# Layer 1's V stage with the expert weights as the moving operand: 128 tokens wide, 32 tokens in four column groups, every second tile as three fp32r products

## The chip, the cores and the metric

The kernel runs on one core of a Trainium2 chip. The core has five engines with queues of their own: TensorE (matmuls into PSUM, called PE in the profile, its weight loads PEld), VectorE (DVE), ScalarE (ACT), GpSimd (POOL) and SyncE (SP), and 16 DMA engines that move data between the chip's memory and SBUF. The metric is the time of one execution in microseconds, as the median of several runs. Everything is f32 unless said otherwise; a matmul on f32 operands leaves two records of TensorE in the trace, one on fp32r operands (f32 rounded so that one pass does it) leaves one.

## The reference, cut to what matters

Two layers; each is a mixer (convolution and attention, not touched here) and then a layer of experts. For each of 272 tokens a router picks 8 x 16 = 128 of 16384 experts. An expert is a row of `u` and a row of `v`, of 1024 numbers each:

```python
def block(args):
    xb, ib, wb = args
    a = jnp.einsum('ted,td->te', u_table[ib], xb)
    act = jax.nn.gelu(a) * wb
    return jnp.einsum('te,ted->td', act, v_table[ib])
...
h = h + _peer(_rmsnorm(h, ffn_norm_g[l]), peer_wq[l], peer_keys[l], peer_u[l], peer_v[l])
...
return h[:, N_META:]
```

The output is the last layer's `h` without the 16 meta tokens: 256 tokens of 1024 numbers.

## The kernel before

**Two ways for the experts.** In each layer a part of the tokens takes the sparse way: for each of them (a job) POOL gathers its 128 rows of `u` and `v` (1 MB) into a buffer `gb`, one of four; VectorE multiplies by the token and sums (L1385), ACT applies gelu and the weight (L1395, L1396), and VectorE adds the weighted `v` rows to `va` (L1371), one job later. Layer 1 has 96 such jobs, in groups of 64 and 32 tokens (`toks`). The other N = 160 tokens (d0 = 112 to 271) take the dense way: all 16384 experts are computed. The U stage multiplies 128 tiles of `u` by the tokens and applies gelu and the routing weights; its result is X and Xh, for each tile j of 128 experts a block `xj(j)` of 128 experts x 160 tokens. The V stage multiplies X by `v`: 128 tiles j of 128 experts x 1024 outputs.

**The V stage.** For each tile j it runs eight matmuls, one for each block c of 128 output columns: the stationary operand is `w_[:, c*128:(c+1)*128]`, a piece of `v`, the moving operand is `xj(j)`, 160 tokens, and the result is added up in PSUM with outputs on partitions and tokens along the row (`pov`, in four tiles `po`). 124 tiles run in a loop; the last four (LJ = 124 to 127) are kept for the end, where they run block by block, so that each block of outputs can be finished while the next is multiplied. In layer 1 a finished block is added to the residual `hT` on VectorE (L1501), turned by two TensorE transposes (L1482), copied out of PSUM (L1487, L1489) and written to `out` in pieces of 128 KB.

**Weights.** All weight tiles come in one order, two tiles j in each transfer of 1 MB, through a ring of four buffers `wraw` (RAW = 4). SP issues a transfer when TensorE is done with the buffer that it overwrites (`dma_to`, L87). `next_w` hands out the next tile, `peek_w(n)` looks n tiles ahead.

**Order.** The order on every engine is that in which the code is written. Between the matmuls of two tiles, `some_gathers(rv)` advances the sparse jobs by a fixed number of steps, three steps to a job; rv is chosen so that the jobs of the layer run out three tiles before the loop's end. In the V stage a gather is issued behind a tiny POOL copy (`warm`, L1359) that waits for the weights of the current tile to land. When a group of sparse tokens is done, `sum_heads` adds up its partial sums by eight matmuls with `zs_` (a matrix that sums partitions) into PSUM `xp`, and `put_back` adds these to `hT`.

**Three products.** Earlier stages already use this: `high` copies a weight tile to fp32r on ACT (L674), `low` subtracts that from the tile on VectorE (L684), and `three` multiplies high by high, low by high and high by low.

Of the kernel before, what the change touches and what calls it, by code (L numbers as in the profile page):

```python
# [7 lines left out]
F32 = mybir.dt.float32  # L8
F32R = mybir.dt.float32r
# [28 lines left out]
GB = 4  # L38
LASTP = 2
# [11 lines left out]
def trunk_kernel(ctx: ExitStack, tc: tile.TileContext, a: dict, out: bass.AP, dbg=None, stop=None):  # L51
    nc = tc.nc
    V, S, G, PE = nc.vector, nc.scalar, nc.gpsimd, nc.tensor

    ctx.enter_context(tc.manual_schedule())
    pp = ctx.enter_context(tc.tile_pool(name="persist", bufs=1))

    def mm(o, l, r, start, stop):
        PE.matmul(o, l, r, start=start, stop=stop, skip_group_check=True)  # L59
# [12 lines left out]
    RAW = 4  # L72
    raws = {}
    first = []
    state = {"dma": 0, "use": 0}
    n_l = len(srcs) // NL
    early_ = [[l * n_l + 30 + p for p in EARLY] for l in range(NL)]
    ring = [k for k in range(len(srcs)) if k not in early_[0] + early_[1]]

    def dma_to(n):  # L80
        while state["dma"] < min(n, len(ring)):
            k = ring[state["dma"]]
            r = pp.tile([128, 2, 1024], F32, name="wraw", bufs=RAW)
            if k == 0:
                first.append(r)
            else:
                nc.sync.dma_start(r, srcs[k])  # L87
# [34 lines left out]
    ident = pp.tile([128, 128], F32, name="ident")  # L122
# [29 lines left out]
    zs_ = {}  # L152
# [10 lines left out]
    def run_all(g):  # L163
        for _ in g:
            pass
# [32 lines left out]
    for l in range(NL):  # L198
        last = l == NL - 1
# [59 lines left out]
        else:  # L259

            p = zp.tile([128, 512], F32, name="z", bufs=3)
# [499 lines left out]
        w_, z = next_w(), zp.tile([128, 512], F32, name="z", bufs=3)[:, :T]  # L761
# [118 lines left out]
        xh = pp.tile([128, 8, T], F32, name="xh").bitcast(F32R)  # L880
# [22 lines left out]
        xp = (xh, xl)  # L903
# [196 lines left out]
        toks = [(META + sum(GROUPS[l][:g]), n) for g, n in enumerate(GROUPS[l])] + ([] if last else [(0, 16)])  # L1100
# [16 lines left out]
        xh = pp.tile([128, 8, T], F32, name="xh")  # L1117
        for i in range(16):
# [9 lines left out]
            if i % 3 == 1:  # L1128
                k = next(ahead, None)
# [33 lines left out]
            if 4 <= i < 12:  # L1163
                c = i - 4
# [184 lines left out]
        def gathers():  # L1349

            bufs = {}

            def gather(k):
                if k < len(jobs):
                    i, m = jobs[k]
                    g_ = bufs[k] = gp.tile([128, 2048], F32, name="gb", bufs=GB)
                    if done["v"]:

                        G.tensor_copy(warm[0:1], state["w"][0:1, 0:1])  # L1359
                    G.indirect_dma_start(out=g_, out_offset=None, in_=a[f"uv{l}"],  # L1360
                                         in_offset=bass.IndirectOffsetOnAxis(
                                             ap=iww[i].bitcast(I32)[:, m // 16, 0, m % 16:m % 16 + 1], axis=0))

            def add(i, m, r):
                s_ = m % 16
                m_ = am[i][:, m // 16, s_:s_ + 1]
                if m == 0:
                    vac[i] = gp.tile([128, 1024], F32, name="va", bufs=2)
                    V.tensor_scalar(vac[i], r, m_, None, op0=OP.mult)
                else:  # L1370
                    V.scalar_tensor_tensor(vac[i], r, m_, vac[i], op0=OP.mult, op1=OP.add)  # L1371

            for k in range(GB):
                gather(k)
            yield from x_steps(0)
            nx = iter(())
            for k, (i, m) in enumerate(jobs):
                if m == 4 and i + 1 < len(toks):
                    nx = x_steps(i + 1)
                if m in (4, 10):  # L1380
                    next(nx, None)
                g_ = bufs.pop(k)
                u_, r = g_[:, 0:1024], g_[:, 1024:]
                m_ = am[i][:, m // 16, m % 16:m % 16 + 1]
                V.scalar_tensor_tensor(u_, u_, 1.0, xrs[i], op0=OP.mult, op1=OP.mult, accum_out=m_)  # L1385
                yield
                if k:
                    add(*prev)
                    gather(k - 1 + GB)
                    if m == 3 and i:  # L1390
                        sum_heads(i - 1)
                    if m == 5 and i:
                        put_back(i - 1)
                yield
                S.activation(m_, m_, AF.Gelu_apprx_tanh)  # L1395
                S.activation(m_, m_, AF.Copy, scale=iww[i][:, m // 16, 1, m % 16:m % 16 + 1])  # L1396
                prev = (i, m, r)
                yield
            add(*prev)
# [57 lines left out]
        LJ = 128 - 2 * LASTP  # L1457
        tail = 3
        rv = (3 * nj + 3 - done["n"] - 3 * tail) / (LJ - tail)
        pos = [pV.tile([128, 512], F32, name=f"po{i}") for i in range(4)]  # L1460
        pov = [pos[3 - c // 2][:, c % 2 * 256:c % 2 * 256 + N] for c in range(8)]
        for j in range(LJ):
            w_ = next_w()
            for c in range(8):
                mm(pov[c], w_[:, c * 128:(c + 1) * 128], xj(j), j == 0 and c % 2 == 0, False)
            some_gathers(rv if j < LJ - tail else 3)
        run_all(gs_)
        vs2.close()

        ws_ = [next_w() for _ in range(2 * LASTP)]  # L1470
        if last:
            ov = out.rearrange("o (t p) d -> p (o t) d", p=128)
            ms = ExitStack()
            pm = ms.enter_context(tc.tile_pool(name=f"pm{l}", bufs=1, space=PSUM))
            turned = []

            def turn_out(c):

                if c % 2 == 0:
                    turned[:] = [pm.tile([128, 512], F32, name="pt", bufs=2)[:, 0:256] for _ in range(2)]  # L1480
                for t in range(2):
                    PE.transpose(turned[t][:, c % 2 * 128:c % 2 * 128 + 128], hT[:, c, 16 + t * 128:144 + t * 128], ident)  # L1482
                if c % 2:
                    for t in range(2):
                        ob = gp.tile([128, 2048], F32, name="gb", bufs=GB)[:, 0:256]
                        if t:
                            S.activation(ob, turned[t], AF.Copy)  # L1487
                        else:
                            V.tensor_copy(ob, turned[t])  # L1489
                        (S if t else nc.sync).dma_start(ov[:, t, c // 2 * 256:c // 2 * 256 + 256], ob)  # L1490

        for c in range(8):
            if c == (1 if last else 5):
                sum_heads(len(toks) - 1)
                put_back(len(toks) - 1)
            for j in range(LJ, 128):
                mm(pov[c], ws_[j - LJ][:, c * 128:(c + 1) * 128], xj(j), False, j == 127)
            if last:
                if c > 1:
                    turn_out(c - 2)  # L1500
                V.tensor_add(hT[:, c, d0:], hT[:, c, d0:], pov[c])  # L1501
        if last:
            turn_out(6)
            turn_out(7)
            ms.close()
        else:
            carry = (pov, vs, d0)
        mts.close()
        xhs.close()
        if last:  # L1510
            vs.close()
# [82 lines left out]
```

## Time and profile before

| | us |
|---|---|
| median of three runs (1714.29 to 1715.16) | 1714.66 |
| the profiled execution | 1712.8 |
| its span, first to last instruction | 1711.0 |
| TensorE busy | 1676.9 (98%) |
| VectorE busy | 1163.2 (68%) |
| ScalarE busy | 575.9 (34%) |
| layer 1's V stage, from the first `po` matmul | 1421.57 |
| last copy out of PSUM ends | 1707.85 |

How to read the rows further down: a row of a window gives the stretch, its length, each engine's busy time with its number of records, the clock that TensorE was granted (1.00 is full), the share of time in which the 16 DMA engines were busy, and GB/s. A row of a timeline gives start, duration, engine, line, operation, output<-inputs, shapes and count; neighbours of one kind are merged. In rows on waits stand who waited for whom, the sum in us, how often, and the longest. In groups stand `busy us, mean ns` behind the bar. L59 is the line of the helper through which all matmuls go, so matmuls are told apart by the names of their tiles. The ends of matmuls are modelled, so their pace is read from starts.

### The profile page before, as it was taken

The page shows a single profiled execution, that of the slowest core. Times are in us where ns is not written, and L with a number is a line of the kernel's source. Part 1 is how long each engine was busy: PE and PEld are TensorE (multiplying, and loading weights), DVE is VectorE, ACT ScalarE, POOL GpSimd, SP SyncE. Part 2 cuts the span into 40 slices and gives each one's busy share as a digit, 9 for nine tenths or more (in the row PEclk, how much of TensorE's full clock was granted, in tenths as well). Part 3 has the DMA queues.
Part 4 walks back from the last instruction along what each step waited for, and adds up shares of the span by engine and source line. Part 5 has one row for each costly group of instructions (what it writes and reads, how often), then busy time and mean ns, then how long its engine had stood idle before and what let it go on. Part 6 is the DMA issues. An engine that isn't in the chain of part 4 may idle for free.

```text
span 1711.0 us, 30698 instructions
## 1 busy us (share of the span) xinstructions
PE 1676.9 (98%) x12067; PEld 1593.6 (93%) x12067; DVE 1163.2 (68%) x3005; ACT 575.9 (34%) x1632; POOL 300.4 (18%) x352
## 2 busy tenths in 40 slices
PE   9999999989999999999999989999999999999998
PEld 7688989989999999998986889999999999999998
DVE  6789888888888544444447898888788885333333
ACT  3475623335544111000024666333355441000000
POOL 0000013222112213222300100122221112222120
PEclk9999999999999999999999999999999999999999
DMA  6344777999999999999962556889999999999995
GB/s 241 109 138 160 249 230 304 363 382 420 421 420 420 420 420 415 421 420 412 416 250 98 137 165 246 256 330 360 411 421 423 423 416 419 385 382 391 400 392 203
DMA packets 85520, 568.51 MB, mean 332 GB/s; under 512 B 9592, under 2 KB 14904, under 8 KB 18168
## 3 DMA queue, kind: packets, MB, share of 16 engines
q1 hardware_dynamic: 49776, 338.54, 50.1%
q0 software_dynamic: 34880, 227.41, 34.5%
q8 instruction: 95, 1.56, 0.4%
q10 hardware_dynamic: 720, 0.60, 0.1%
q14 instruction: 49, 0.40, 0.1%
HBM read 556.18 MB, written 1.05 MB: 326 GB/s over the span
## 4 chain that ended last, share of the span: by engine, by line
PE 66%; DMA 10%; DVE 9%; issue 9%; ACT 2%; POOL 2%; POOLq 0%; SPq 0%; DVEq 0%; ACTq 0%
PE po L59 27%; PE A L59 16%; PE z L59 16%; DMA wraw<-vn 6%; DMA gb<-uv,iww 4%; PE aps L59 3%; POOL gb L1360 2%; PE wp L59 1%; DVE va L1371 1%; DVE gb L1385 1%; PE sc L59 1%; PE xp L59 1%; DVE acc L626 0%; DVE xh L684 0%; DVE kh L684 0%
## 5 line engine op out<-in xcount | busy, mean ns | idle before, releaser
L59 PE MATMUL A<-xh,wraw 128*128 128x160 f32 x3776 | 534.8, 301 | 1.2 <-ACT idxT L990 1.2
L1385 DVE SCALAR_TENSOR_TENSOR gb<-gb,xr 128x1024 f32<-128x1024 f32 x208 | 254.6, 1224 | 396.5 <-DMA gb<-uv,iww 396.2
L59 PEld LDWEIGHTS A<-xh,wraw 128*128 128x128 f32 x3776 | 517.7, 191 | 1.6 <-issue 1.6
L1360 POOL DMA_INDIRECT gb<-uv,iww x208 | 225.1, 1082 | 528.5 <-DVE va L1371 381.5
L59 PE MATMUL po<-Xh,wraw 128*128 128x160 f32 x2080 | 286.9, 300 | 3.9 <-DMA wraw<-vn 3.3
L59 PEld LDWEIGHTS po<-Xh,wraw 128*128 128x128 f32 x2080 | 283.1, 190 | 6.6 <-DMA wraw<-vn 5.3
L59 PE MATMUL po<-X,wraw 128*128 128x160 f32 x2016 | 277.1, 300 | 6.5 <-DMA wraw<-vn 3.6
L59 PEld LDWEIGHTS po<-X,wraw 128*128 128x128 f32 x2016 | 274.2, 190 | 8.9 <-DMA wraw<-vn 5.8
L1371 DVE SCALAR_TENSOR_TENSOR va<-gb,am,va 128x1024 f32<-128x1024 f32 x203 | 260.0, 1281 | 1.7 <-ACT am L1396 1.5
L1395 ACT ACTIVATE am<-am 128x1 f32<-128x1 f32 x208 | 41.3, 198 | 591.0 <-DVE gb L1385 590.9
L59 PE MATMUL z<-xg,wraw 128*128 128x272 f32 (+2 forms) x960 | 223.5, 391 | 0.1
L59 PEld LDWEIGHTS z<-xg,wraw 128*128 128x128 f32 (+1 forms) x960 | 175.0, 188 | 38.8 <-issue 5.8
L1299 ACT ACTIVATE ohA<-ohE,wlo 128x128 f16<-128x128 f16 x320 | 105.2, 429 | 6.7 <-DVE ohE L1296 5.9
L1359 POOL COPY warm<-wraw 1x1 f32<-1x1 f32 x86 | 33.2, 386 | 323.7 <-DMA wraw<-vn 323.7
L626 DVE SCALAR_TENSOR_TENSOR acc<-upad,cols,acc 128x272 f32<-128x272 f32 (+1 forms) x198 | 82.8, 487 | 0.2
L1310 ACT ACTIVATE Xh<-wp 128x260 f32<-128x260 f32 (+18 forms) x80 | 25.0, 312 | 125.5 <-DVE Xh L1307 111.1
L1396 ACT ACTIVATE am<-am,iww 128x1 f32<-128x1 f32 x208 | 61.3, 295 | 6.8
L1296 DVE TENSOR_TENSOR ohE<-ioh,idxT 128x512 f16<-128x512 f16 x160 | 60.4, 420 | 0.0
L638 POOL DMA_DIRECT2D part<-cp x12 | 13.2, 1102 | 254.5 <-ACT cp L635 106.6
L59 PE MATMUL wp<-ohE,ohA 128*128 128x128 f16 x640 | 51.1, 219 | 1.8 <-DVE ohA L1297 1.8
L59 PEld LDWEIGHTS <-ohA 128*128 128x128 f16 x640 | 43.2, 97 | 7.0 <-DVE ohA L1297 2.8
L59 PE MATMUL A<-xh,we 128*128 128x160 f32 x320 | 45.3, 299 | 0.0
(423 smaller groups left out, 1912.0 us busy)
## 6 DMA issues: line engine op xcount, KB each, us to landing
wraw<-vn SPq DMA_DIRECT2D x128, 1024.0 KB
wraw<-u SPq DMA_DIRECT2D x118, 1024.0 KB
wraw<-w_in SPq DMA_DIRECT2D x27, 1024.0 KB
wraw<-wq SPq DMA_DIRECT2D x16, 1024.0 KB
we<-u SPq DMA_DIRECT2D x10, 1024.0 KB
wraw<-w_out SPq DMA_DIRECT2D x8, 1024.0 KB
wraw<-w_mla SPq DMA_DIRECT2D x4, 1024.0 KB
wraw<-w_conv SPq DMA_DIRECT2D x4, 1024.0 KB
```

Source lines behind the costliest of these rows:

```text
L59: PE.matmul(o, l, r, start=start, stop=stop, skip_group_check=True)
L626: V.scalar_tensor_tensor(acc[:, c, t0:], u_, weight(c, k), acc[:, c, t0:], op0=OP.mult, op1=OP.add)
L638: G.dma_start(part[:, :, t0:], u_[:, :, t0:], accum_op=OP.add)
L1296: V.tensor_tensor(E[q], ioh[:, None].to_broadcast(full), pairs(q, b), op=OP.is_equal)
L1299: S.activation(A_[1][:, t // 2, :, t % 2], E[0][:, t // 2, :, t % 2], AF.Copy, scale=wlo[:, 4 * b + t:4 * b + t + 1])
L1310: S.activation(x_, p[:, :, a:b].rearrange("p t j -> p j t"), AF.Copy, scale=1.0 / WS)
L1359: G.tensor_copy(warm[0:1], state["w"][0:1, 0:1])
L1360: G.indirect_dma_start(out=g_, out_offset=None, in_=a[f"uv{l}"], in_offset=bass.IndirectOffsetOnAxis(ap=iww[i].bitcast(I32)[:, m // 16, 0, ...
L1371: V.scalar_tensor_tensor(vac[i], r, m_, vac[i], op0=OP.mult, op1=OP.add)
L1385: V.scalar_tensor_tensor(u_, u_, 1.0, xrs[i], op0=OP.mult, op1=OP.mult, accum_out=m_)
L1395: S.activation(m_, m_, AF.Gelu_apprx_tanh)
L1396: S.activation(m_, m_, AF.Copy, scale=iww[i][:, m // 16, 1, m % 16:m % 16 + 1])
```

## The change

Layer 0 stays as it is. In layer 1's V stage the operands change places: X becomes the stationary operand and `v` the moving one, so that the result stands with tokens on partitions and outputs along the row.

- *wide*: 128 of the 160 tokens (columns 32 to 159 of `xj(j)`) are stationary, and two matmuls of 512 columns each give all 1024 outputs, into `po[0]` and `po[1]`.
- *narrow*: the other 32 tokens are stationary in four column groups, each with 256 of the 1024 outputs, into four strips of 32 partitions of `po[2]`. This is done for four tiles at a time, behind every fourth tile.
- *three parts*: every odd tile from 3 to 123 has its wide part as three fp32r products. `split`, written three tiles ahead, makes `ah` and `hi` on ACT and `al` and `lo` on VectorE; `hi` and `lo` have two sets of buffers, the storage `xh` and the new tiles `vh`, `vl`.
- *a fifth weight buffer*: every fifth `v` tile pair of layer 1 goes to `wr5` in a new pool; transfers are issued at every fourth tile.
- *the residual* is added by matmuls of `hT` with the identity, for the dense tokens in mid-loop and for the sparse ones in `give`, which takes the place of `sum_heads`; `give_out` takes that of `put_back` and writes the finished tokens to `out`.
- *the end*: the last four tiles' narrow parts, the last `give`, then the wide parts of the first and the second 512 outputs, with copies and writes behind each. There are no transposes and no additions into `hT` any more.

```diff
+            v = k - n_l * NL + 64
+            if v >= 0 and v % 5 == 4:
+                r = state["pool"].tile([128, 2, 1024], F32, name="wr5")
+            else:
+                r = pp.tile([128, 2, 1024], F32, name="wraw", bufs=RAW)
...
+            def three_parts(j):
+
+                return 3 <= j < LJ and j % 2 == 1
...
+                w_ = peek_w(2)
+                if j // 2 % 2:
+                    hi, lo = [tpp.tile([128, 1024], F32, name=x).bitcast(F32R) for x in ("vh", "vl")]
+                else:
+                    hi, lo = [axy[:, 1024 * x:1024 * x + 1024].bitcast(F32R) for x in range(2)]
+                ah, al = [tpp.tile([128, 128], F32, name=x, bufs=2).bitcast(F32R) for x in ("ah", "al")]
+                S.activation(ah, xj(j)[:, 32:160], AF.Copy)
+                S.activation(hi, w_, AF.Copy)
+                V.tensor_tensor(al, xj(j)[:, 32:160], ah.bitcast(F32), op=OP.subtract)
+                V.tensor_tensor(lo, w_, hi.bitcast(F32), op=OP.subtract)
...
+                for h in hs:
+                    mm(po[h], a_, w_[:, 512 * h:512 * h + 512], s0, end)
...
+                for g in range(4):
+                    mm(po[2][32 * g:32 * g + 32, 0:256], a_[:, 0:32], w_[:, 256 * g:256 * g + 256], s0, end)
...
+                for g in range(k):
+                    mm(p[n * g:n * g + n], zs_[n], vac[i][:, w * g:w * g + w], True, False)
+                for x in range(w // 128):
+                    for g in range(k):
+                        mm(p[n * g:n * g + n, 128 * x:128 * x + 128], hT[:, g * w // 128 + x, q0:q0 + n], ident,
+                           False, x == w // 128 - 1)
...
-            for c in range(8):
-                mm(pov[c], w_[:, c * 128:(c + 1) * 128], xj(j), j == 0 and c % 2 == 0, False)
-            some_gathers(rv if j < LJ - tail else 3)
...
+                if j % 4 == 0:
+                    dma_to(ring.index(state["use"] // 2) + RAW + 1)
+                w_ = next_w()
+                four.append((j, w_))
+                if three_parts(j):
+                    hi, lo, ah, al = cut.pop(j)
+                    for a_, b in ((ah, hi), (al, hi), (ah, lo)):
+                        wide(a_, b, (0, 1))
+                else:
+                    wide(xj(j)[:, 32:160], w_, (0, 1), j == 0)
+                if j % 4 == 3:
+                    for x, y in four:
+                        narrow(xj(x), y, x == 0)
+                    four = []
...
+                if three_parts(j + 3):
+                    split(j + 3)
+                some_gathers(rv if j < LJ - tail else 3)
```

What stands on TensorE at the loop's end and behind it, before (out<-in by tile names, with the output's partitions and columns; `x4` is four in a row):

```order
L59 MATMUL po_12766<-Xh,wraw 128x160 x4
L59 MATMUL xp<-zs_123,va 128x32 x8
L59 MATMUL po_12766<-Xh,wraw 128x160 x4
L59 MATMUL po_12765<-Xh,wraw 128x160 x4
L1482 MATMUL pt<-ident,hT 128x128 x2
L59 MATMUL po_12765<-Xh,wraw 128x160 x4
L1482 MATMUL pt<-ident,hT 128x128 x2
```

and now, from the last odd tile of the loop on:

```order
L59 MATMUL po_12768<-vh,ah 128x512
L59 MATMUL po_12769<-vh,ah 128x512
L59 MATMUL po_12768<-vh,al 128x512
L59 MATMUL po_12769<-vh,al 128x512
L59 MATMUL po_12768<-vl,ah 128x512
L59 MATMUL po_12769<-vl,ah 128x512
L59 MATMUL po_12770<-wraw,Xh 32x256 x32
L59 MATMUL xp<-va,zs_123 32x256 x4
L59 MATMUL xp<-ident,hT 32x128 x8
L59 MATMUL po_12768<-wraw,Xh 128x512 x4
L59 MATMUL po_12769<-wraw,Xh 128x512 x4
```

Eight 160-column matmuls a tile, with transposes between blocks, have become six of 512 columns (two in an even tile), a narrow block for four tiles and the ends of two halves; the narrow row with `x32` holds two blocks, that of the loop's last four tiles and that of tiles 124 to 127.

On VectorE, in the middle of the loop, before: only the products (`gb`) and additions (`va`) of the gathers take turns.

```order
L1385 SCALAR_TENSOR_TENSOR gb,am_9854<-gb,xr 128x1024
L1371 SCALAR_TENSOR_TENSOR va<-gb,am_9854,va 128x1024
L1385 SCALAR_TENSOR_TENSOR gb,am_9854<-gb,xr 128x1024
L1371 SCALAR_TENSOR_TENSOR va<-gb,am_9854,va 128x1024
L1385 SCALAR_TENSOR_TENSOR gb,am_9854<-gb,xr 128x1024
```

Now, at a place in the second half of the loop:

```order
L1389 SCALAR_TENSOR_TENSOR gb,am_9854<-gb,xr 128x1024
L1486 TENSOR_TENSOR al<-Xh,ah 128x128
L1487 TENSOR_TENSOR vl<-wraw,vh 128x1024
L1375 SCALAR_TENSOR_TENSOR va<-gb,am_9854,va 128x1024
L1486 TENSOR_TENSOR al<-Xh,ah 128x128
L1487 TENSOR_TENSOR xh<-wr_14270,xh 128x1024
L1389 SCALAR_TENSOR_TENSOR gb,am_9854<-gb,xr 128x1024
L1375 SCALAR_TENSOR_TENSOR va<-gb,am_9854,va 128x1024
```

The two subtractions of every second tile have come between the products and additions; `xh` and `vl` are the two sets for `lo` in turn.

On SP, the weight transfers of layer 1's V stage were one row, `wraw<-vn` 64 times; now every fifth goes to the new buffer:

```order
L91 DMA wraw<-vn 128x2048 x4
L91 DMA wr_12773<-vn 128x2048
L91 DMA wraw<-vn 128x2048 x4
L91 DMA wr_12945<-vn 128x2048
L91 DMA wraw<-vn 128x2048 x4
```

What moved there is only the place that every fifth transfer goes to; the order of the tiles is the same.

More of the change, by code (lines that the diff above doesn't have):

```diff
@@ L1390, in gathers @@
                     if m == 3 and i:
-                        sum_heads(i - 1)
+                        (give if last else sum_heads)(i - 1)
                     if m == 5 and i:
-                        put_back(i - 1)
+                        (give_out if last else put_back)(i - 1)
                 yield
@@ L1459, in trunk_kernel @@
         rv = (3 * nj + 3 - done["n"] - 3 * tail) / (LJ - tail)
[L1460 to L1463, printed above, removed]
-            for c in range(8):
-                mm(pov[c], w_[:, c * 128:(c + 1) * 128], xj(j), j == 0 and c % 2 == 0, False)
-            some_gathers(rv if j < LJ - tail else 3)
-        run_all(gs_)
-        vs2.close()
@@ L1470, in trunk_kernel @@
[L1470 to L1490, printed above, removed]
@@ L1492, in trunk_kernel, with split, wide, narrow @@
-        for c in range(8):
[L1493 to L1506, printed above, removed]
+        if last:
+            mts.close()
+            tps = ExitStack()
+            tpp = state["pool"] = tps.enter_context(tc.tile_pool(name="tp", bufs=1, side="right"))
+            axy = pp.tile([128, 8 * T], F32, name="xh")
+            po = [pV.tile([128, 512], F32, name=f"po{i}") for i in range(3)]
+            cut = {}
+            def three_parts(j):
+                return 3 <= j < LJ and j % 2 == 1
+            def split(j):
+                w_ = peek_w(2)
[8 more added lines that the diff above has]
+                V.tensor_tensor(lo, w_, hi.bitcast(F32), op=OP.subtract)
+                cut[j] = hi, lo, ah, al
+            def wide(a_, w_, hs, s0=False, end=False):
+                for h in hs:
+                    mm(po[h], a_, w_[:, 512 * h:512 * h + 512], s0, end)
+            def narrow(a_, w_, s0=False, end=False):
+                for g in range(4):
+                    mm(po[2][32 * g:32 * g + 32, 0:256], a_[:, 0:32], w_[:, 256 * g:256 * g + 256], s0, end)
+            def give(i):
+                q0, n = toks[i]
+                k = 128 // n
+                w = 1024 // k
+                p = pG.tile([128, 512], F32, name="xp")[:, 0:w]
+                for g in range(k):
[4 more added lines that the diff above has]
+                           False, x == w // 128 - 1)
+                done["p"] = p
+            def give_out(i):
+                q0, n = toks[i]
+                k = 128 // n
+                w = 1024 // k
+                ob = gp.tile([128, 1024], F32, name="xs")[:, 0:w]
+                S.activation(ob, done["p"], AF.Copy)
+                for g in range(k):
+                    S.dma_start(out[0, q0 - META:q0 - META + n, w * g:w * g + w], ob[n * g:n * g + n])
+            four = []
+            for j in range(LJ):
+                if j % 4 == 0:
[11 more added lines that the diff above has]
+                        narrow(xj(x), y, x == 0)
+                    four = []
+                if j == LJ // 2:
+                    for c in range(8):
+                        mm(po[c // 4][:, c % 4 * 128:c % 4 * 128 + 128], hT[:, c, 144:272], ident, False, False)
+                    for x in range(2):
+                        for g in range(4):
+                            mm(po[2][32 * g:32 * g + 32, 128 * x:128 * x + 128], hT[:, 2 * g + x, 112:144], ident,
+                               False, False)
+                if three_parts(j + 3):
+                    split(j + 3)
+                some_gathers(rv if j < LJ - tail else 3)
+            run_all(gs_)
+            vs2.close()
+            ws_ = [next_w() for _ in range(2 * LASTP)]
+            for j in range(LJ, 128):
+                narrow(xj(j), ws_[j - LJ], False, j == 127)
+            give(len(toks) - 1)
+            ob = gp.tile([128, 2048], F32, name="gb", bufs=GB)[:, 0:256]
+            V.tensor_copy(ob, po[2][:, 0:256])
+            for g in range(4):
+                nc.sync.dma_start(out[0, 96:128, 256 * g:256 * g + 256], ob[32 * g:32 * g + 32])
+            for h in range(2):
+                for j in range(LJ, 128):
+                    wide(xj(j)[:, 32:160], ws_[j - LJ], (h,), False, j == 127)
+                if h == 0:
+                    give_out(len(toks) - 1)
+                for x in range(2):
+                    ob = gp.tile([128, 2048], F32, name="gb", bufs=GB)[:, 0:256]
+                    if x:
+                        S.activation(ob, po[h][:, 256:512], AF.Copy)
+                    else:
+                        V.tensor_copy(ob, po[h][:, 0:256])
+                    (S if x else nc.sync).dma_start(
+                        out[0, 128:256, 512 * h + 256 * x:512 * h + 256 * x + 256], ob)
+            tps.close()
+        else:
+            pos = [pV.tile([128, 512], F32, name=f"po{i}") for i in range(4)]
+            pov = [pos[3 - c // 2][:, c % 2 * 256:c % 2 * 256 + N] for c in range(8)]
+            for j in range(LJ):
+                w_ = next_w()
+                for c in range(8):
+                    mm(pov[c], w_[:, c * 128:(c + 1) * 128], xj(j), j == 0 and c % 2 == 0, False)
+                some_gathers(rv if j < LJ - tail else 3)
+            run_all(gs_)
+            vs2.close()
+            ws_ = [next_w() for _ in range(2 * LASTP)]
+            for c in range(8):
+                if c == 5:
+                    sum_heads(len(toks) - 1)
+                    put_back(len(toks) - 1)
+                for j in range(LJ, 128):
+                    mm(pov[c], ws_[j - LJ][:, c * 128:(c + 1) * 128], xj(j), False, j == 127)
@@ L1507, in trunk_kernel @@
             carry = (pov, vs, d0)
-        mts.close()
+            mts.close()
         xhs.close()
```

1 line of the change is left out of this document (removed).

## The prediction

> **What bounds the kernel now.** I read the chain of waits first: which work ended last, by engine and by line.
>
> ```profile
> PE 66%; DMA 10%; DVE 9%; issue 9%; ACT 2%; POOL 2%; POOLq 0%; SPq 0%; DVEq 0%; ACTq 0%
> PE po L59 27%; PE A L59 16%; PE z L59 16%; DMA wraw<-vn 6%; DMA gb<-uv,iww 4%; PE aps L59 3%; POOL gb L1360 2%; PE wp L59 1%; DVE va L1371 1%; DVE gb L1385 1%; PE sc L59 1%; PE xp L59 1%; DVE acc L626 0%; DVE xh L684 0%; DVE kh L684 0%
> ```
>
> TensorE carries it, and the largest share is `po`, the V stage of both layers. The same chain in order of time, over the stage that the change rewrites:
>
> ```profile
> 1421.57 82.85 PE po L59 x608
> 1504.42 1.73 PE xp L59 x16
> 1506.15 188.05 PE po L59 x1384
> 1694.20 1.70 PE xp L59 x16
> ```
>
> An f32 matmul leaves two records: 128 tiles of 8 matmuls are 2048 records, of which 608 + 1384 = 1992 stand here and 56 behind. One takes 188.05/1384 = 0.136 us, so a tile of 16 takes 2.18 us. The loop of 124 tiles ends 8 records before 1694.20, at 1693.1: 271.5 us. Nothing but TensorE is on the chain here. The waits of the same stretch agree, and the DMA's share is the next thing to look at:
>
> ```profile
> SPq L87 <- PE po L59: 239.6, 60, 5.7
> POOL warm L1359 <- DMA wraw<-vn: 176.6, 36, 9.2
> DVE gb L1385 <- DMA gb<-uv,iww: 163.2, 38, 7.2
> ...
> core 0: us, PE busy (x) PEld busy (x) DVE busy (x) ACT busy (x) POOL busy (x), PEclk, DMA share, GB/s
> 1421.60:1693.10 271.50, 271.50 (x2002) 271.50 (x2003) 98.98 (x123) 20.20 (x82) 56.35 (x73) 1.00 0.97 386
> 1421.60:1687.00 265.40, 265.40 (x1957) 265.40 (x1958) 98.98 (x123) 20.20 (x82) 56.35 (x73) 1.00 0.98 392
> 580.00:860.00 280.00, 272.81 (x1986) 268.94 (x1985) 124.13 (x155) 27.18 (x105) 73.70 (x98) 1.00 1.01 418
> ```
>
> The weight queue waits for TensorE to give buffers back, POOL's gathers wait for weights, VectorE waits for gathers: all hang on TensorE. The DMA is close behind: up to 1687 it moves 265.4 x 392 = 104.0 MB, and layer 0's V stage shows 418 GB/s held for 280 us. At 418 the same bytes take 249 us. So there are some 22 us between TensorE's time and the DMA's, and a change to TensorE alone can win about that in this loop.
>
> **The change part by part.** All durations are of the profiled execution (1712.8 us, span 1711.0); the median of the three timed runs is 1714.66, 1.9 above it, and I carry the difference over.
>
> *Wide matmuls.* 512 columns of f32 stand at one place, and 272 at many:
>
> ```profile
> 229.18 3.83 PE L59 MATMUL z<-xg,wraw 128*128 128x272 f32 x16
> 232.85 0.38 PE L59 MATMUL sc<-uk,qr 128*128 128x128 f32 x2
> ...
> 923.38 0.30 PEld L59 LDWEIGHTS aps<-un 128*128 128x128 f32 x2 [0.45 <-issue]
> ...
> 923.38 2.09 PE L59 MATMUL aps<-un 128*128 128x512 f32 x4
> ...
> L59 PE MATMUL aps<-un 128*128 128x512 f32 x8 | 4.3, 618 | 0.0
> ```
>
> 272 columns take (232.85 - 229.18)/16 = 0.229 us a record and 160 take 0.136, so a column costs 0.00083 us and 512 columns come to 0.229 + 240 x 0.00083 = 0.43. From the four records of 512 themselves: the last begins about 0.6 us before the end, which leaves 1.49 us for three steps, 0.50 each at most; with the first two weight loads (0.30) taken off, as nothing ran beside them, 0.40. I take 0.43, where the slope lies, with 0.40 and 0.50 as ends. A plain tile has two matmuls, four records: 1.72 us. There are 63 such tiles (0, 1, 2 and the even ones): 108.4 us.
>
> *Three products.* Earlier stages already multiply in fp32r, one record a matmul:
>
> ```profile
> 1003.90 0.28 PE L59 MATMUL z<-un,wq 128*128 128x256 f32 x1
> ...
> 1005.08 0.28 PE L59 MATMUL z<-uk,wq 128*128 128x256 f32 x1
> ```
>
> Ten steps in 1.18 us are 0.118 for 256 columns; 512 lie between 0.215 (half of the f32 pair's 0.43) and 0.236 (twice 0.118); I take 0.225. Six a tile are 1.35 us, and 61 tiles 82.4 us.
>
> *Narrow matmuls.* Layer 0 has one burst of the kind, four column groups of 32 with two records each, 128 columns:
>
> ```profile
> 217.72 0.42 PE L59 MATMUL scm<-uk,qm 128*32 128x128 f32 x8
> 218.07 0.64 PE L59 MATMUL z<-g,sq 128*128 128x272 f32 x3
> ...
> 217.71 0.16 PEld L59 LDWEIGHTS scm<-uk,qm 128*32 128x32 f32 x8
> ...
> 228.74 0.61 PE L59 MATMUL sc<-uk,qr 128*128 128x128 f32 x4
> ```
>
> Full-width records of 128 columns come every (229.18 - 228.74)/4 = 0.11 us; eight in a row would be 0.88, but the burst is over after 218.07 - 217.72 = 0.35. That is two rounds side by side (0.22) and 0.13 for the switch. 256 columns take 0.216 by the slope above, so a tile has two rounds, 0.43, and a block of four tiles 1.73 + 0.13 = 1.86. 31 blocks: 57.7 us. Bounds: no switch cost 0.43 a tile, one for every tile 0.56.
>
> The Trainium skill, "TensorE: Matmul & The Clock Gate", section "Measured speedup vs the span model", gives 2.38 times for three column groups, 79% of full overlap; that would make a tile 0.54 us instead of 0.46 and the sum 10 us more. The burst above has no room for it unless the switch cost is none.
>
> *Small additions.* Adding hT in mid-loop: 8 x 0.22 + 0.43 + 0.13 = 2.3 us. The first group's `give` (two groups of 64, 512 wide; then 128-wide rounds): 0.86 + 0.86 + 0.13 = 1.9, where sum_heads took 1.73.
>
> TensorE's loop: 108.4 + 82.4 + 57.7 + 2.3 + 1.9 = 252.7 us against 271.5: **18.8 less**.
>
> *The split on ACT and VectorE* is new work beside the matmuls. Its price is in earlier lines, which do the same to weights:
>
> ```profile
> L674 ACT ACTIVATE wq<-wraw 128x1024 fp32r<-128x1024 f32 x24 | 25.2, 1050 | 2.7 <-PE aps L59 1.6 <-PE z L59 1.1
> L684 DVE TENSOR_TENSOR wq<-wraw,wq 128x1024 fp32r<-128x1024 f32 x10 | 12.3, 1225 | 2.8 <-ACT wq L674 2.8
> L1385 DVE SCALAR_TENSOR_TENSOR gb<-gb,xr 128x1024 f32<-128x1024 f32 x208 | 254.6, 1224 | 396.5 <-DMA gb<-uv,iww 396.2
> L1371 DVE SCALAR_TENSOR_TENSOR va<-gb,am,va 128x1024 f32<-128x1024 f32 x203 | 260.0, 1281 | 1.7 <-ACT am L1396 1.5
> ```
>
> 1.05 us on ACT and 1.22 on VectorE, and the 128-column pieces some 0.3 each: 61 x 1.5 = 92 us on VectorE beside 99 that it had, 191 of 257; ACT gets 82 beside 20. The split of tile j+3 stands in the program at tile j, and its buffers are those of tile j-1, so it begins when TensorE is done with j-1: 0.3 + 1.05 + 1.22 = 2.6 us, while TensorE has j, j+1 and j+2 (1.72 + 1.35 + 1.72 = 4.8). I cost it at nothing; the cover is 2.2 us, 4.0 where a narrow block lies between. Behind it on VectorE stand gather products, and a late gather in front of a split uses that cover up.
>
> *Weights.* Blocks of four tiles hold two buffers until their end, and the fifth buffer `wr5` makes up for one of them: up to three transfers are open while two are in use. SP waits for the block's end, then issues two. With 249 us of DMA against 252.7 of TensorE neither hides the other fully. Layer 0's stage is the nearest case; between nothing and its 7.2 us of idle TensorE in 280 I take 4.
>
> *The end.* Before, from 1693.1 to 1711.0: 17.9 us, of which the last piece is
>
> ```profile
> 1707.47 0.38 ACT L1487 ACTIVATE gb<-pt 128x256 f32<-128x256 f32 x1 [0.75 <-PE pt L1482]
> 1707.88 0.35 ACTq L1490 DMA_DIRECT2D out<-gb  x1
> ```
>
> 3.15 us from the copy's end (1707.85) to the end of the span. After: one narrow block 1.86, the last `give` 0.43 + 0.43 + 0.13 = 1.0, eight wide matmuls 6.9, drain 0.2, copy 0.4, and 3.15: 13.5. No transposes and no additions into hT on VectorE between them: **4.4 less**. The copies and writes of the other parts lie beside the wide matmuls.
>
> Sum: -18.8 + 4 - 4.4 = -19.2 us, 1693.6 for a profiled execution, **1695.5** for the median.
>
> **The rivals.**
>
> *The transfers get no faster* than this stage's 392 GB/s. The last tile then lands at 1687.0 as now, and the end's 13.5 us follow: span 1700.5, median 1704.2. For it: the share is already 0.98. Against: layer 0's 418.
>
> *512 columns cost the upper 0.50.* 252 records x 0.07 = 17.6 us more: 1713.1, no change to be told.
>
> *The gathers become the bound, and it is slower.* VectorE ran ahead of TensorE before; now every split ties it to tile j-1, and gather k+3 is issued only behind the additions of job k. The cycle of three jobs is the gather's time from issue to use and some 4.5 us on VectorE and POOL (product 1.22, split 1.5, addition 1.28, issue 0.5). That time has been
>
> ```profile
> 708.33 0.96 POOL L1360 DMA_INDIRECT gb<-uv,iww  x1 [1.80 <-DVE va L1371]
> 721.52 1.23 DVE L1385 SCALAR_TENSOR_TENSOR gb<-gb,xr 128x1024 f32<-128x1024 f32 x1 [2.53 <-DMA gb<-uv,iww]
> ...
> 1510.18 0.97 POOL L1360 DMA_INDIRECT gb<-uv,iww  x1 [0.16 <-DVE va L1371]
> 1530.39 1.23 DVE L1385 SCALAR_TENSOR_TENSOR gb<-gb,xr 128x1024 f32<-128x1024 f32 x1 [7.21 <-DMA gb<-uv,iww]
> ```
>
> 13.2 us in layer 0 and 20.2 here (each gather's product is the third behind its issue). At 13.2 a job takes 5.9 us, and 39 jobs 230: covered. At 20.2 it takes 8.2, the loop 321: 45 slower, 1760. It decides from 16.8, where 39 x 7.1 = 277 eats loop and end alike. Against: in layer 0, where the DMA is fullest, it is the short one; the long one comes with gathers that were issued far ahead.
>
> *The column groups take turns.* 8 x 0.216 = 1.73 a tile instead of 0.46: 157 us more, 1853. The burst's 0.35 us speaks against it. The Trainium skill, same page, section "The mechanism", says that a weight load overlaps running matmuls only where the row group differs, and here all four share their rows; by that rule each narrow load would stand between matmuls. The eight loads in 0.16 us disagree.
>
> **How the numbers follow.** Forecast 0.66; slow transfers 0.12; dear wide matmuls 0.06; gathers 0.12; turns 0.04. The forecast's own ends: with narrow at 0.43, fp32r at 0.215 and no waits, 4.0 + 3.7 + 4 less, 1684; with a switch for every tile, 93 x 0.13 = 12 more, 1708. The range takes that, slow transfers and dear wide matmuls in: 1683 to 1713. A change of 0.2%, 3.4 us, is about what a measurement of this kernel can tell from none. Faster: forecast and slow transfers, 0.78. Same: dear wide matmuls and a gather time near 16.8, 0.08. Slower: the rest, 0.14.
>
> **What would show it.** 512-column f32 records start every 0.43 us, fp32r ones every 0.22; a narrow block takes 1.9; TensorE's waits in the loop are a few us, for `wraw` or for `vl`/`xh`; the stage's DMA is near 415 GB/s; the last wide matmul ends 3.8 us before the end. Wrong, if VectorE's waits for gathers stand in front of splits and TensorE waits for VectorE tens of us, if the DMA stays at 392, or if a narrow block takes 7 us.

## The result, and the profile after

The changed kernel takes **1700.27 us** (median of 6 runs, 1698.29 to 1702.97), the kernel before 1714.58 in the same comparison (6 runs, 1713.34 to 1715.57). The ratio is 0.9916, with a 95% interval of 0.9904 to 0.9929: 0.7 to 1.0% faster. The forecast was 1695.5, with a range of 1683 to 1713. The profiled execution took 1700.04 us, with a span of 1698.3.

The chain of waits of the changed kernel, in order of time, over the rewritten stage (start, us, engine, tile, line, count):

```profile
1422.58 78.21 PE po L59 x476
1500.79 1.88 PE xp L59 x20
1502.67 183.31 PE po L59 x1198
1685.98 0.87 PE xp L59 x24
1686.85 7.08 PE po L59 x16
...
1693.95 0.44 DVE gb L1570
...
1694.41 0.38 ACT gb L1568
```

As before, nothing but TensorE stands there until the last copies. The last loop block's end lies inside the third row: behind the loop come the 32 narrow records of tiles 124 to 127, at 0.0556 us each (from the rows below) 1.78 us. So the loop runs from 1422.58 to 1684.2, **261.6 us** where it took 271.5, and the end, from there to 1698.3, takes **14.1** where it took 17.9. The stage begins 1.0 us later than before (1422.58 against 1421.57). No line of the change reaches what stands ahead of it, and in the runs below, whose code up to there is the same, it begins anywhere from 1421.8 to 1426.5. So -9.9 - 3.8 + 1.0 = -12.7 is the difference of the two spans.

The pace is read from the starts in TensorE's timeline of the changed kernel (start, duration, tiles, shapes, count):

```profile
1505.90 1.07 PE L59 MATMUL po<-wraw,X 128*32 128x256 f32 x16
1506.79 1.05 PE L59 MATMUL po<-wr,X 128*32 128x256 f32 x16
1507.76 1.98 PE L59 MATMUL po<-wraw,X 128*128 128x512 f32 x4
1509.18 1.02 PE L59 MATMUL po<-xh,ah 128*128 128x512 f32 x2
1510.05 0.63 PE L59 MATMUL po<-xh,al 128*128 128x512 f32 x2
1510.51 0.63 PE L59 MATMUL po<-xh,ah 128*128 128x512 f32 x2
...
1513.15 0.63 PE L59 MATMUL po<-vh,al 128*128 128x512 f32 x2
1513.62 0.62 PE L59 MATMUL po<-vl,ah 128*128 128x512 f32 x2
1514.17 3.85 PE L59 MATMUL po<-wraw,X 128*32 128x256 f32 x36
...
1687.75 0.19 PEld L59 LDWEIGHTS po<-wraw,Xh 128*128 128x128 f32 x1 [0.24 <-issue]
...
1688.18 0.19 PEld L59 LDWEIGHTS po<-wraw,Xh 128*128 128x128 f32 x1 [0.24 <-issue]
```

- A 512-column f32 record takes 0.43 us: the weight loads of the wide matmuls at the end stand 1688.18 - 1687.75 apart. A plain tile takes 1.72.
- Two fp32r records take 1510.51 - 1510.05 = 0.46 to 1513.62 - 1513.15 = 0.47, so one 0.2325, and a tile of six 1.395.
- In a narrow block, 16 records take 1506.79 - 1505.90 = 0.89 us, 0.0556 each: a round of four groups in 0.222.
- From one narrow block to the next it is 1514.17 - 1505.90 = 8.27 us. Two plain tiles (3.44) and two of three products (2.79) leave **2.04** for a narrow block: 32 records of 0.0556 are 1.78, and the other 0.26 are the change to column groups and back. (Single starts around such a change shift by a few tenths; from block to block these shifts are the same and cancel.)

The waits of the changed kernel over the rewritten stage, and its windows over the loop:

```profile
ACT ah L1484 <- PE po L59: 128.9, 56, 4.0
POOL gb L1364 <- DVE al L1486: 120.9, 22, 9.7
...
POOL gb L1364 <- DVE va L1375: 69.3, 15, 7.1
...
ACT vh L1485 <- DMA wraw<-vn: 10.8, 9, 3.0
ACT xh L1485 <- DMA wraw<-vn: 7.2, 5, 2.8
```

```profile
1422.60:1684.10 261.50, 261.50 (x1666) 146.53 (x1670) 183.34 (x244) 95.82 (x205) 54.90 (x74) 1.00 0.98 402
...
1423.00:1680.00 257.00, 257.00 (x1623) 143.86 (x1622) 178.95 (x240) 95.11 (x203) 54.74 (x74) 1.00 1.00 407
```

No wait of TensorE for a transfer or a split stands in the list, but for one of 0.2 us of a weight load. ACT's splits wait for TensorE (`ah`, 56 times), POOL's gathers for VectorE, and 18 us of ACT's waits are for weights. VectorE's 163.2 us of waiting for gathers are gone from the list: what it waits for now is ACT's part of the splits (75 us in the same list), and a gather has landed before its product is due.

### The profile page after: what moved, and what is told of

The parts are those of the page before. It is cut to its first block, busy times and chain, and to the rows that moved or that the text cites. A ratio compares the mean times of both kernels' runs of the same rounds, so it can differ in the third digit from the quotient of the medians.

```text
span 1698.3 us, 30386 instructions
## 1 busy us (share of the span) xinstructions
PE 1668.1 (98%) x11705; PEld 1465.7 (86%) x11705; DVE 1244.3 (73%) x3116; ACT 651.8 (38%) x1754; POOL 301.8 (18%) x352
## 4 chain that ended last, share of the span: by engine, by line
PE 66%; DMA 10%; DVE 10%; issue 9%; ACT 2%; POOL 2%; POOLq 0%; SPq 0%; DVEq 0%; ACTq 0%
PE po L59 27%; PE z L59 17%; PE A L59 17%; DMA wraw<-vn 6%; DMA gb<-uv,iww 4%; PE aps L59 3%; POOL gb L1364 2%; PE wp L59 1%; DVE va L1375 1%; DVE gb L1389 1%; PE sc L59 1%; PE xp L59 0%; DVE acc L630 0%; DVE xh L688 0%; DVE upad L688 0%
## 5 line engine op out<-in xcount | busy, mean ns | idle before, releaser
L1364 POOL DMA_INDIRECT gb<-uv,iww x208 | 229.4, 1103 | 696.0 <-DVE va L1375 436.8
L59 PE MATMUL po<-Xh,wraw 128*128 128x160 f32 x1040 | 144.6, 300 | 2.9 <-DMA wraw<-vn 2.7
L59 PEld LDWEIGHTS po<-Xh,wraw 128*128 128x128 f32 x1040 | 141.7, 190 | 5.3 <-DMA wraw<-vn 5.3
L59 PE MATMUL po<-X,wraw 128*128 128x160 f32 x1008 | 141.7, 302 | 4.5 <-DMA wraw<-vn 2.4
L59 PEld LDWEIGHTS po<-X,wraw 128*128 128x128 f32 x1008 | 138.9, 192 | 6.9 <-DMA wraw<-vn 4.7
L59 PE MATMUL po<-wraw,Xh 128*32 128x256 f32 (+1 forms) x536 | 78.9, 428 | 0.0
L59 PE MATMUL po<-wraw,X 128*32 128x256 f32 (+1 forms) x516 | 76.4, 429 | 0.5 <-ACT gl L1424 0.5
L59 PEld LDWEIGHTS po<-wraw,Xh 128*32 128x32 f32 (+1 forms) x536 | 32.7, 126 | 32.4 <-issue 24.3
L59 PEld LDWEIGHTS po<-wraw,X 128*32 128x32 f32 (+1 forms) x516 | 31.3, 126 | 31.9 <-issue 23.5
L642 POOL DMA_DIRECT2D part<-cp x12 | 13.2, 1104 | 255.3 <-ACT cp L639 106.8
```

What stands on the lines that cost most here:

```text
L642: G.dma_start(part[:, :, t0:], u_[:, :, t0:], accum_op=OP.add)
```

## The experiments

Each experiment was compared with the kernel before once more, and its ratio is to that time. The kernel before took 1713.97 us (17 runs) beside the all-plain tiles, the blocks of two tiles, the 80 tiles and the four buffers; 1713.84 us (11 runs) beside the old order, the single column group and the two with spread jobs; and 1714.21 us (9 runs) beside the two with halved gathers.

### What the change of places is worth without the three products

```
             def three_parts(j):
-                return 3 <= j < LJ and j % 2 == 1
+                return False
```

> All tiles plain: no split, no fp32r products; everything else as after the change. Theory (TensorE's own time is the stage): an odd tile goes from six fp32r matmuls at 0.2325 us (1.395) to four f32 records at 0.43 (1.72), 61 tiles x 0.325 = 19.8 us more, about 1720 us, slower than the kernel before the change. Rival (the DMA, 104 MB at up to 420 GB/s, or VectorE's splits set the pace, so taking the splits away costs little): at most 5 us more, 1705 us.

Measured: 1719.32 us (1718.86 to 1721.83), ratio 1.0035, interval 1.0022 to 1.0048: **slower than before**, by 5.4 us. From its chain (the first and the last row of TensorE in the loop), from its waits and from its windows:

```profile
1421.94 84.06 PE po L59 x440
...
1705.15 0.87 PE xp L59 x24
```

```profile
DVE gb L1389 <- DMA gb<-uv,iww: 169.9, 38, 10.5
```

```profile
1423.00:1680.00 257.00, 257.00 (x1403) 113.39 (x1402) 89.27 (x112) 18.90 (x75) 59.13 (x73) 1.00 0.96 383
```

1705.15 - 1421.94 - 1.78 = 281.4 us of loop, by its pace 124 x 1.72 + 31 x 2.04 + 4.2 = 280.7. The old order took 271.5: a tile of eight 160-column matmuls is 2.18, a wide part with its share of a narrow block 1.72 + 0.51 = 2.23. So the change of places alone costs TensorE time, and what wins is the three products: 1719.3 - 1700.3 = 19.0 us over 61 tiles, 0.31 each, where 1.72 - 1.395 = 0.325 was to be had. In the profiled executions its loop is 9.9 us longer than the old one, and its end, 13.6 us instead of 17.9, gives 4.3 back. VectorE waits for gathers again, as before the change: what ended those waits is the split.

### Three products in the old order

The kernel before, with its eight 160-column matmuls a tile, and every odd tile as 24 fp32r matmuls with splits of the same kind:

```
+                if three_parts(j):
+                    hi, lo, ah, al = cut.pop(j)
+                    for c in range(8):
+                        s_ = slice(c * 128, c * 128 + 128)
+                        mm(pov[c], hi[:, s_], ah, False, False)
+                        mm(pov[c], lo[:, s_], ah, False, False)
+                        mm(pov[c], hi[:, s_], al, False, False)
```

> The kernel before the change (v stationary, 160 tokens moving, four weight buffers, old end), with every odd tile of layer 1's V stage from 3 to 123 as three fp32r products, split on ACT and VectorE as in the change. It asks whether the operands had to change places for the three products to pay. Theory A (a record takes its columns and a little: 0.118 us at 256 columns, 0.0005 a column, so 0.073 at 160): 24 records, 1.75 us a tile instead of 2.18, 61 tiles, 26 us less on TensorE; then the transfers hold it at some 257 us for the loop, about 1700 us. Theory B (128 stationary columns have to be loaded for every record, and that sets a floor of some 0.11 us, the pace of 128-column matmuls in the trace of before): 24 x 0.11 = 2.64 us a tile, 28 us more, about 1742 us.

Measured: 1744.06 us (1743.93 to 1745.91), ratio 1.0179, interval 1.0166 to 1.0192: 30 us slower than before, as theory B had it. TensorE's timeline there, from one plain tile to the next:

```profile
1503.84 2.38 PE L59 MATMUL po<-X,wraw 128*128 128x160 f32 x16
1505.94 0.35 PE L59 MATMUL po<-ah,vh 128*128 128x160 f32 x1
...
1508.70 2.37 PE L59 MATMUL po<-X,wraw 128*128 128x160 f32 x16
```

From plain tile to plain tile it is 1508.70 - 1503.84 = 4.86 us. Without the 2.18 of the plain one that leaves 2.68 for 24 fp32r records, 0.112 each. By their columns (0.2325 x 160/512) they would take 0.073. 61 x (2.68 - 2.18) = 30.5 us, which is the whole loss.

That TensorE's weight loads count as busy for all 257 us of a window of 257 does not say what sets this pace: in the kernel before they are busy all the time as well (the prediction's window of 271.50), at one load a record too, and there the records follow their columns. The trace of the kernel before says more, in rows with few moving columns:

```profile
85.38 0.56 PE L59 MATMUL aps<-kh,xh 98*16 98x16 f32 x16
...
868.76 1.85 PE L59 MATMUL xp<-zs,va 128*128 128x16 f32 x16
870.46 3.51 PE L59 MATMUL po<-Xh,wraw 128*128 128x160 f32 x24
```

With 128 stationary columns, records of 16 moving columns come every (870.46 - 868.76)/16 = 0.106 us, those of 32 every 1.70/16 = 0.106 and those of 64 every 1.73/16 = 0.108 (the `xp` rows of the prediction's chain). With 16 stationary columns (and 98 rows) all sixteen records are over in 0.56 us, 0.035 each at most. So the pace of short records does not follow the moving columns; it goes with the width of the stationary operand, which is what a load has to bring in. That it is the load itself is inferred from this. At 160 columns an f32 record takes 0.136 us and covers a load; an fp32r one would take 0.073 and does not. So the operands had to change places before the three products could win: with 512 columns behind each load, the 0.2325 us of the matmul is the longer.

### The narrow matmuls: side by side, and the price of a block

Once with all narrow matmuls in the first column group (its outputs in the first 32 partitions of two banks; the additions of `hT` in mid-loop and the last copy of the narrow part follow them there):

```
-                    mm(po[2][32 * g:32 * g + 32, 0:256], a_[:, 0:32], w_[:, 256 * g:256 * g + 256], s0, end)
+                    mm(po[2 + g // 2][0:32, g % 2 * 256:g % 2 * 256 + 256], a_[:, 0:32],
+                       w_[:, 256 * g:256 * g + 256], s0 and g % 2 == 0, end)
```

> As after the change, but the four narrow matmuls of a tile all use the first column group (same 32 partitions, two PSUM banks) instead of four. Theory (the groups run side by side): a tile's narrow part goes from 0.45 to 8 x 0.216 = 1.73 us, 128 tiles, 164 us more, about 1864 us. Rival (they take turns anyway): no change, 1700 us.

Measured: 1870.47 us, one run, 170 above the changed kernel. Its timeline on TensorE, from one narrow block, with the plain tile behind it (36 records together), to the next:

```profile
1500.46 9.01 PE L59 MATMUL po<-wraw,X 128*32 128x256 f32 x36
1508.90 0.80 PE L59 MATMUL po<-xh,ah 128*128 128x512 f32 x1
...
1513.90 7.09 PE L59 MATMUL po<-wraw,X 128*32 128x256 f32 x32
```

From block to block it is 1513.90 - 1500.46 = 13.44 us. Less the 3.44 and 2.79 of the plain and the three-product tiles, a block takes 7.21: its records start 0.216 us apart, 6.91 for 32, and 0.30 are the change of shape. With four groups the records came every 0.0556: 3.9 times as fast inside the block, 3.5 times with the change of shape in it (7.21 / 2.04). The Trainium skill, "TensorE: Matmul & The Clock Gate", section "The mechanism", has weight loads overlap running matmuls only where the row group differs. The trace does not bear that out: all four groups share their rows here, and four matmuls with their four loads took 0.222 us, about the 0.216 that one alone took. The Trainium skill, same page, section "Measured speedup vs the span model", gives 2.38 times for three groups, 79% of three; here it is 3.5 of 4, 88%.

Then with a narrow block behind every second tile, 62 blocks of 16 records in place of 31 of 32:

```
-                if j % 4 == 3:
+                if j % 2 == 1:
                     for x, y in four:
```

> Narrow blocks behind every second tile instead of every fourth: 31 more blocks, the same number of narrow matmuls. By the trace after the change a block costs 0.26 us beyond its matmuls (switch in and out): 31 x 0.26 = 8 us more, about 1708 us. By the 0.13 of the prediction: 4 us more, 1704 us.

Measured: 1709.45 us (1707.59 to 1711.28), ratio 0.9972, interval 0.9961 to 0.9984. 31 more blocks cost 9.2 us, **0.30 each**. The chain (the first row of the stage and the first behind the loop) says the same:

```profile
1422.16 82.16 PE po L59 x492
...
1695.53 0.87 PE xp L59 x24
```

1695.53 - 1422.16 = 273.4 against 263.4, 10.0 us over 31 blocks, 0.32 each. The prediction had 0.13 from a single burst; 0.26 from the pace and 0.30 from this run and from the single group's blocks agree better with each other than with that.

### More tiles as three products: the next bound

80 tiles instead of 61, the two sets of buffers taken in turn by a counter:

```
-                return 3 <= j < LJ and j % 2 == 1
+                return 3 <= j < LJ and j % 3 != 0
...
-                if j // 2 % 2:
+                made[0] += 1
+                if made[0] % 2:
```

> Three products on two of three tiles (80 tiles instead of 61), two sets of buffers in turn, written three tiles ahead. Theory (TensorE's own time): 19 more tiles x 0.325 = 6.2 us less, about 1694 us, TensorE without waits. Rival (VectorE's cover is used up: it goes to some 223 us of 255, and a split may begin only one to two tiles ahead of its use): TensorE waits for the split's low part, 1700 us or more.

Measured: 1700.39 us (1696.62 to 1702.25), ratio 0.9919, interval 0.9906 to 0.9932, where the theory had 1694. Nineteen more tiles at 0.325 less are 6 us that TensorE did not need and that did not come off. The chain shows who took them (the start and the end of the loop and two of the legs between, the second without its end), and the window how fast the transfers ran:

```profile
1423.05 56.55 PE po L59 x352
...
1535.39 79.94 PE po L59 x540
1615.40 10.69 DMA wr<-vn
...
1626.17 1.07 ACT xh L1487
1627.26 1.24 DVE xh L1489
...
1628.55 35.83 PE po L59 x236
1664.44 10.13 DMA wraw<-vn
...
1685.64 1.08 PE xp L59 x24
```

```profile
1423.00:1680.00 257.00, 255.97 (x1680) 152.10 (x1684) 202.50 (x276) 118.61 (x239) 67.52 (x74) 1.00 1.00 408
```

The chain leaves TensorE: a transfer of 10.7 us lands, ACT and VectorE split it, and only then TensorE goes on. The loop takes 1685.64 - 1423.05 - 1.78 = 260.8 us. The rival had the time right, but its cause is not shown by that. The chain can be read in two ways: the bytes come too slowly, or splits and VectorE stand in each other's way. So the same kernel, and the change itself, once more with less to transfer: every gather issued in layer 1's V stage brings half of its row.

```
+                    half[k] = last and done["v"]
-                    G.indirect_dma_start(out=g_, out_offset=None, in_=a[f"uv{l}"],
+                    G.indirect_dma_start(out=g_[:, 0:1024] if half[k] else g_, out_offset=None,
+                                         in_=a[f"uv{l}"].rearrange("n (h d) -> (n h) d", h=2) if half[k] else a[f"uv{l}"],
...
-                u_, r = g_[:, 0:1024], g_[:, 1024:]
+                u_, r = g_[:, 0:1024], g_[:, 0:1024] if half[k] else g_[:, 1024:]
```

> Two of three tiles as three products, and every gather that layer 1 issues during its V stage brings only half its row (4 KB a partition instead of 8), so that about 20 of the stage's 104 MB are not moved; the sparse result of these jobs is not the reference's. All engine work stays. Theory: with two of three the stage is held by its transfers (408 GB/s), so without these bytes TensorE's own time shows: 44 plain tiles at 1.72, 80 at 1.395, 31 narrow blocks at 2.04 and 4.2 of mid-loop work are 254.7 us against 261.5, so about 1693 to 1694 us. Rival: the splits and VectorE's order hold it, not the bytes; then it stays at 1699 to 1701.

> The change as it is, with the same halved gathers in layer 1's V stage (4 KB a partition instead of 8; the sparse result of these jobs is not the reference's). Theory: TensorE sets the changed kernel's loop and waits for nothing, so the bytes are free there and the time stays within 2 us of the changed kernel's 1700.3. Rival: the transfers already slow it in places that the profiled execution does not show; then it falls by 3 us or more.

Measured: two of three, halved: **1694.79 us** (1694.49 to 1695.02), ratio 0.9884, interval 0.9869 to 0.9899. The change, halved: **1700.54 us** (1699.88 to 1701.91), ratio 0.9917, interval 0.9904 to 0.9931. The chain and the window of the first:

```profile
1424.16 76.57 PE po L59 x486
1500.73 1.88 PE xp L59 x20
1502.61 178.66 PE po L59 x1226
1681.27 0.87 PE xp L59 x24
```

```profile
1423.00:1680.00 257.00, 256.47 (x1717) 154.29 (x1719) 207.75 (x282) 118.07 (x244) 66.84 (x74) 1.00 0.86 335
```

With fewer bytes (335 GB/s over the window instead of 408) the same splits, at no lower load on VectorE (207.8 us beside 202.5), let TensorE run through: the loop takes 1681.27 - 1424.16 - 1.78 = 255.3 us, where TensorE's own time was reckoned at 254.7, and the 6 us are there. So transfers hold the version with 80 tiles, and TensorE holds the change: with some 19 of its 104 MB taken away its loop takes the same 261.6 us (1424.43 to 1687.84 on its chain, less 1.78). The change stands close to the point where the two are equal.

Both kernels were also tried with the sparse jobs spread to the loop's end, since the last leg of the 80-tile version's chain runs through additions on VectorE:

```
-        tail = 3
+        tail = 0 if last else 3
```

> As after the change, but the sparse jobs are spread evenly over the whole loop instead of nine steps in its last three tiles. In the trace after the change VectorE's last addition ends about 1 us before TensorE needs it, so theory: no change, 1700 us within 2. Rival (the bunched steps hold up the last splits): 2 to 4 us less, 1697 us.

> Three products on two of three tiles, with the sparse jobs spread evenly. In the run without the spreading TensorE waited 2.3 us for VectorE's last addition, and four times for a split whose transfer came 10 to 15 us after its issue. Theory (the end of VectorE's queue took the gain): 2.3 us or more less than that run, 1697 us or below. Rival (the transfers hold it): 1700 us.

Measured: the change with this, 1699.92 us (1697.25 to 1701.67), ratio 0.9917, interval 0.9904 to 0.9929: no difference. The 80 tiles with this: 1698.95 us (1695.88 to 1705.95), ratio 0.9914, interval 0.9898 to 0.9931. The chain of the latter has lost its last leg through VectorE, and has four legs through transfers all the same; the last two:

```profile
1607.16 11.68 DMA wraw<-vn
...
1641.74 10.82 DMA wraw<-vn
```

Theory and rival of the 80 tiles lie close together, and the time came between them; that the transfers hold it rests on the halved gathers, not on this run. None of the three kernels that move all their bytes (the 80 tiles, and both with the jobs spread) can be told from the change.

### The fifth weight buffer

The ring without `wr5`, and with one transfer less ahead:

```
-            if v >= 0 and v % 5 == 4:
+            if False:
...
-                    dma_to(ring.index(state["use"] // 2) + RAW + 1)
+                    dma_to(ring.index(state["use"] // 2) + RAW)
```

> The fifth weight buffer taken away, blocks of four tiles kept: two transfers open at most while two buffers are held. Theory (the fifth buffer is needed, since two transfers of 1 MB at half of 420 GB/s take 10 us and a block of four tiles 8.3): about 1.7 us of waiting for weights a block, 31 blocks, up to 50 us more, 1750 us. Rival (the transfers are early enough without it): no change, 1700 us.

Measured: 1709.72 us (1703.3 to 1713.81, 11 runs), ratio 0.9975, interval 0.9963 to 0.9986: 9.5 us more than the change, between the theory's 50 and the rival's none. From the waits and the windows:

```profile
ACT xh L1485 <- DMA wraw<-vn: 70.8, 28, 4.9
ACT vh L1485 <- DMA wraw<-vn: 55.9, 28, 4.3
...
PE po L59 <- DMA wraw<-vn: 3.4, 6, 1.0
```

```profile
1423.00:1680.00 257.00, 254.06 (x1590) 140.90 (x1593) 170.60 (x231) 92.00 (x195) 58.62 (x73) 1.00 0.97 393
```

ACT waits 127 us for weights instead of 18, and TensorE has its first waits, 3.4 us for the weights themselves; the stage's rate is 393 GB/s where it was 407. On the chain three late transfers of 9 to 12 us release TensorE directly, and a fourth releases a split. The theory had 1.7 us of waiting in each of 31 blocks; from block to block only seven stretches are longer than in the change, by 0.15 to 1.3 us. The buffer, with the transfer that it lets run ahead, is worth 9.5 us, two thirds of what the change wins. In the profiled executions 6.6 us of that are in the loop (268.2), and 1.5 lie ahead of the stage.

## Why the prediction was right, point by point

Direction, mechanism and range held; the time came out 4.8 us above the forecast. In spans: 1711.0 - 18.8 + 4 - 4.4 = 1691.8 was foretold, 1698.3 came, 6.5 more.

- *Wide matmuls, 63 x 1.72 = 108.4.* As foretold: 0.43 a record, where 0.40 and 0.50 were the ends. The rival of 0.50 fell.
- *Three products, 61 x 1.35 = 82.4.* Mis-sized: a record takes 0.2325, near the upper end given (0.236), 1.395 a tile and 85.1 in all. 2.7 us.
- *Narrow blocks, 31 x 1.86 = 57.7.* The largest mis-sized term: the rounds were right (0.222 against 0.216 each), but the change of shape costs 0.26 to 0.30 and not 0.13. 31 x 2.04 = 63.2. 5.5 us. The prediction took 0.13 as the rest of a burst of eight records between two starts; but the timeline shows starts near a change of shape shifted by a few tenths, so two starts of different shapes do not carry a price of that size. That the groups run side by side held; the rival in which they take turns had put 157 us on it, and it fell (one group costs 170 us more).
- *Mid-loop additions, 2.3 + 1.9.* The `give` stands in the chain at 1.88. With the terms above the loop is 260.9, and 261.6 was measured. Part of the 0.7 lies here: from narrow block to narrow block the timeline has 8.28 us, 10.36 where the `give` stands between and 10.84 where `hT` is added, which makes 2.1 and 2.6.
- *Waits, 4 us.* None. The loop is some 8.9 us longer than the 252.7 reckoned, so TensorE asks for the same bytes more slowly, and they come in time. The prediction's two errors took part of each other away, and that is luck. Had the other terms been right, 4 us would probably have been too little: the 80-tile version, whose own time on TensorE is 254.7, took 260.8, 6 us more, and came no further than the change.
- *The end, 13.5.* 14.1. The step held, a saving of 3.8 instead of 4.4. The last two copies stand one behind the other on the chain (0.44 and 0.38), where the prediction had one of 0.4.
- *The split at no cost.* Held, with the fifth buffer: ACT waits for TensorE, not TensorE for a split. Without the buffer ACT waits 127 us for weights, and the cover goes in places.
- *Transfers no faster than 392.* Fell in the change as it stands: 407 over the window, 402 over the loop. But it was near: the 80-tile version is held by its transfers, at 408 GB/s, below the 418 that the prediction took from layer 0.
- *Gathers become the bound.* Fell: no wait of VectorE for a gather is left in the list, and halving the gathers changed nothing in the change. The ties of VectorE to TensorE are there as described (POOL waits 190 us for VectorE, ACT 129 for TensorE), but a gather takes less than its cycle leaves it.

The stage's start 1.0 us later makes up the rest: 2.7 + 5.5 + 0.7 (loop above its terms) - 4 + 0.6 + 1.0 = 6.5.

## What to carry to other kernels

Three fp32r products in place of one f32 matmul pay only where the matmul behind each weight load is long enough: they lose 30 us at 160 columns and win 19 at 512, so look at the shape of the moving operand before splitting a matmul. Put narrow matmuls in column groups into blocks, and price each block by a change of shape taken from a long regular stretch, not from two starts beside each other. When two limits lie within a few per cent, as TensorE and transfers here, take bytes away from both versions in an experiment: it shows at once which of them holds which.

## What the runs showed of the hardware that was not expected

- A change from full width to column groups and back costs 0.26 us by the pace and 0.30 by doubling the blocks; to a single column group and back it is 0.30.
- A change between f32 and fp32r costs nothing that shows: with no fp32r in the loop a cycle of four tiles is (281.4 - 4.2) / 31 = 8.94 us, which leaves 8.94 - 4 x 1.72 = 2.06 for the narrow block, against 2.04 with it.
- fp32r records of 160 columns come every 0.112 us, those of 512 columns every 0.2325; f32 records of 16, 32 and 64 columns come every 0.106 to 0.108. Of f32 and fp32r records with 128 stationary columns, none here came faster than that. Where the limit lies for fp32r wasn't measured; an estimate from 512 columns, 0.112/0.2325 x 512, is about 250 columns.
- With 80 tiles, where the transfers hold the loop, they ran at 408 GB/s in this stage, not at layer 0's 418. What takes the rest stays open.
